# Two transformer blocks on one core: a feed-forward in three parts, with nine of 22 tile pairs as seven half-size products

## The chip, the cores and the metric

The kernel runs on one core of a Trainium2 chip. The metric is the device time in microseconds (us) of one execution. TensorE (PE) multiplies, VectorE (DVE) and ScalarE (ACT) work element by element, GpSimd (POOL) does a few copies, and SyncE (SP) issues most transfers; ScalarE and GpSimd can issue transfers too, each from a queue of its own.

## The reference

A sequence of 512 tokens with 1024 features goes through two blocks, in float32. The first block has three branches (a recurrent one, a latent attention, a differential attention with a position bias), a gated merge, an output product and a convolutional feed-forward. The second block has two layers; each is feed-forward, mixer, feed-forward:

```python
n = _modulate(_rmsnorm_2(h, norm_g[l, 0]), mod[:, 0, 0], mod[:, 0, 1])   # x * (1 + scale) + shift
h = h + 0.5 * mod[:, 0, 2] * _swiglu(n, ffn_w_in[l, 0], ffn_w_out[l, 0])

def _swiglu(x, w_in, w_out):                 # w_in 1024 x 5632, w_out 2816 x 1024
    a, b = jnp.split(x @ w_in, 2, axis=-1)
    return (jax.nn.silu(a) * b) @ w_out
```

`mod` comes from a vector c times `ada_w` (1024 x 9216 for each layer).

## The kernel before

Activations lie transposed: features on the 128 partitions in KD = 8 chunks, S = 512 tokens along a row. Each float32 operand is held as a pair `hi` + `lo` of float32r tiles; `mm3` multiplies three of the four combinations, so a 128 x 128 block of weights costs three matmuls of 512 columns. `weight` loads 128 x 1024 weights into `raw` (three buffers), makes `hi` on ScalarE and `lo = raw - hi` on VectorE (four buffers each). While the flag `spare` is set, every other `lo` is made on GpSimd.

`dense` makes one output tile of 128 features. `dense_halves` makes the first four of a stage in two halves of 256 tokens, so that they can start when the norm of the first half is there. `outputs` makes the last product of a stage and gathers the statistics of the next norm; its last tile (two tiles where the inner size is 8 chunks) is made in halves, and `part` computes the first half's norm factors during the second. `scaled` applies a norm.

`swiglu` has NF = 22 pairs of a gate tile and a value tile; `hh`, `hl` hold all 22 results, then 8 down tiles of 22 chunks each follow. There are four such feed-forwards, at about 1089, 1850, 2230 and 2970 us of the span. In each pair the gate goes through silu (L740), is multiplied with the value (L741) and split (L344, L346). `modulation` puts 72 products of `ada_w` (one 128 x 1024 transfer into `raw` and one VectorE operation, L1436) for each layer into a list from which `filler` takes them.

Order: a list scheduler places instructions on each engine's queue ahead of time by the order of the program, among those that it takes to be ready; a filler's instructions get a much lower priority. Each engine then works strictly through its own queue.

In the first block `filler` also interleaves the products that don't depend on a branch: `spilled` and `gates` write them to memory (`gates` after a tanh on ScalarE), and `gated` reads them back through SP's queue. `merge` sums the three gated branches; five of its eight tiles have two branches summed ahead (MERGED).

## Time and profile before

| | |
|---|---|
| median of 3 runs | 3353.23 us (3349.75 to 3354.49) |
| profiled execution | 3352.4 us, its span 3350.6 us |
| mean granted TensorE clock | 0.992 |
| TensorE busy | 98% of the span |
| VectorE, ScalarE, GpSimd busy | 57%, 40%, 2% |

The span runs from the first to the last instruction. Busy time of TensorE counts overlapping matmuls once, so a busy TensorE can still run below its rate: there the spacing of matmul starts is read from the timeline, and the granted clock from the windows.

### The profile page before, as it was taken

Reading aid. Unit: us, or ns where it says so; the run is one execution under the profiler, and the core shown is the slowest. Engines: PE = TensorE matmul, PEld = TensorE weight load, DVE = VectorE, ACT = ScalarE, POOL = GpSimd, SP = SyncE. Lnnn points to the kernel's source line nnn. Section 1 sums busy time; section 2 is a strip of 40 time slices with the busy share of each in tenths; the row PEclk is TensorE's granted clock in tenths of the full one; section 3 lists DMA queues with packets and bytes.
Section 4 is the critical chain, followed back from the end, with each engine's and each line's share of the span. In section 5 each row is a group of like instructions: output and inputs, shape, how many; then the busy total and the mean of one; then the engine's idle time right before and its main releaser. Section 6 shows DMA issues by size and latency. Waiting matters only on the chain.

```text
span 3350.6 us, 43133 instructions
## 1 busy us (share of the span) xinstructions
PE 3278.2 (98%) x16534; PEld 2724.2 (81%) x16534; DVE 1921.9 (57%) x3628; ACT 1346.7 (40%) x2365; POOL 79.7 (2%) x124
## 2 busy tenths in 40 slices
PE   8999998999999999999999999999999999999998
PEld 6779777788888888887787888898888878788887
DVE  6757685777664644368656644454444875653333
ACT  4646664444432322248632322232222774332321
POOL 0000121000000000000000000000000000000000
PEclk9999999999999999999999999999999999999999
DMA  5351225454453444441235444444443322423332
GB/s 180 94 148 36 81 90 177 154 153 156 139 170 122 138 149 136 146 127 61 88 108 186 137 139 148 143 125 140 149 150 125 94 76 89 153 89 100 95 93 71
DMA packets 144922, 415.00 MB, mean 124 GB/s; under 512 B 28005, under 2 KB 32933, under 8 KB 144202
## 3 DMA queue, kind: packets, MB, share of 16 engines
q1 hardware_dynamic: 142248, 408.02, 38.4%
q0 software_dynamic: 2176, 3.97, 0.5%
q8 instruction: 130, 2.13, 0.3%
q14 instruction: 78, 0.64, 0.1%
q10 hardware_dynamic: 290, 0.24, 0.0%
HBM read 383.06 MB, written 27.01 MB: 122 GB/s over the span
## 4 chain that ended last, share of the span: by engine, by line
PE 88%; DVE 5%; ACT 4%; DMA 2%; issue 1%; SPq 0%; DVEq 0%; ACTq 0%; POOL 0%; POOLq 0%
PE acc L277 25%; PE acc L279 25%; PE acc L278 25%; PE o L822 2%; PE s L783 2%; PE t L810 1%; PE s L278 1%; PE s L277 1%; PE s L279 1%; ACT hi L268 1%; DVE lo L272 1%; PE t L425 1%; DMA raw<-in_ada_dram 1%; PE s L1562 0%; ACT sq L1505 0%
## 5 line engine op out<-in xcount | busy, mean ns | idle before, releaser
L277 PE MATMUL acc<-xh,hi 128*128 128x512 f32 (+1 forms) x2872 | 1084.3, 381 | 17.1 <-ACT gst L627 3.6
L278 PE MATMUL acc<-xl,hi 128*128 128x512 f32 (+1 forms) x2872 | 1088.2, 381 | 2.5 <-DVE xl L348 1.2
L268 ACT ACTIVATE hi<-raw 128x1024 fp32r<-128x1024 f32 (+2 forms) x529 | 541.4, 1024 | 1361.4 <-PE acc L278 1247.0
L279 PE MATMUL acc<-xh,lo 128*128 128x512 f32 (+1 forms) x2872 | 1086.4, 381 | 1.1 <-DVE lo L272 1.1
L272 DVE TENSOR_TENSOR lo<-raw,hi 128x1024 fp32r<-128x1024 f32 (+1 forms) x513 | 613.0, 1196 | 462.3 <-ACT hi L268 440.0
L277 PEld LDWEIGHTS acc<-xh,hi 128*128 128x128 f32 x2872 | 541.1, 189 | 121.9 <-ACT gst L627 5.5
L278 PEld LDWEIGHTS acc<-xl,hi 128*128 128x128 f32 x2872 | 542.5, 189 | 101.1 <-issue 3.9
L279 PEld LDWEIGHTS acc<-xh,lo 128*128 128x128 f32 x2872 | 542.6, 189 | 98.6 <-issue 3.7
L1436 DVE CUSTOM_DVE_ANT_0 raw<-raw,sc,vp 128x1024 f32<-128x1024 f32 x144 | 184.9, 1284 | 269.4 <-DMA raw<-in_ada_dram 268.8
L279 PE MATMUL acc<-hh,lo 128*128 128x512 f32 (+1 forms) x880 | 338.0, 384 | 0.0
L278 PE MATMUL acc<-hl,hi 128*128 128x512 f32 (+1 forms) x880 | 334.5, 380 | 0.0
L277 PE MATMUL acc<-hh,hi 128*128 128x512 f32 (+1 forms) x880 | 333.0, 378 | 0.0
L278 PEld LDWEIGHTS acc<-hl,hi 128*128 128x128 f32 x880 | 165.2, 188 | 37.9
L277 PEld LDWEIGHTS acc<-hh,hi 128*128 128x128 f32 x880 | 165.1, 188 | 34.7
L279 PEld LDWEIGHTS acc<-hh,lo 128*128 128x128 f32 x880 | 165.4, 188 | 33.2
L741 DVE TENSOR_TENSOR g<-g,acc 128x512 f32<-128x512 f32 x84 | 57.8, 688 | 218.7 <-PE acc L279 217.8
L726 DVE SCALAR_TENSOR_TENSOR res<-acc,mod,res 128x512 f32<-128x512 f32 (+1 forms) x48 | 33.9, 707 | 120.0 <-PE acc L279 120.0
L346 DVE TENSOR_TENSOR ptl<-t,pth 128x512 fp32r<-128x512 f32 (+3 forms) x148 | 80.7, 566 | 29.8 <-ACT pth L344 28.8
L787 ACT ACTIVATE pr<-pr,mx 128x128 f32<-128x128 f32 (+3 forms) x160 | 88.7, 556 | 18.3 <-DVE mx L786 16.3
L786 DVE CUSTOM_DVE_ANT_0 pr<-s,cm 128x128 f32<-128x128 f32 (+3 forms) x160 | 75.0, 486 | 23.9 <-PE s L783 16.0
L344 ACT ACTIVATE pth<-t 128x512 fp32r<-128x512 f32 (+3 forms) x148 | 69.6, 496 | 40.4 <-PE t L810 37.3
L810 PE MATMUL t<-cm,pr 128*128 128x128 f32 x400 | 72.8, 276 | 2.5 <-DVE pr L796 2.5
(522 smaller groups left out, 4091.8 us busy)
## 6 DMA issues: line engine op xcount, KB each, us to landing
raw<-in_w_in_dram SPq DMA_DIRECT2D x176, 512.0 KB, 3.6
raw<-in_ada_dram SPq DMA_DIRECT2D x144, 512.0 KB, 3.5
raw<-in_w_out_dram SPq DMA_DIRECT2D x64, 512.0 KB, 3.5
raw<-in_w_mix_dram SPq DMA_DIRECT2D x56, 512.0 KB, 3.5
raw<-in_w_up_dram SPq DMA_DIRECT2D x44, 512.0 KB, 3.9
gd<-gst SPq DMA_DIRECT2D x56, 256.0 KB, 2.3
gt<-gd SPq DMA_DIRECT2D x56, 256.0 KB, 3.2
raw<-in_w_gate_dram SPq DMA_DIRECT2D x24, 512.0 KB, 4.1
```

The source lines that it names most:

```text
L268: self.last_act = nc.scalar.activation(hi[:, :n], raw[:, :n], AF.Copy)
L272: nc.vector.tensor_sub(lo[:, :n], raw[:, :n], hi[:, :n].bitcast(F32))
L277: return [mm(acc, ahi, bhi, start=start, stop=False, **kw), mm(acc, ahi, blo, start=False, stop=False, **kw), mm(acc, alo, bhi, start=Fals ...
L278: mm(acc, ahi, blo, start=False, stop=False, **kw),
L279: mm(acc, alo, bhi, start=False, stop=stop, **kw)]
L344: nc.scalar.activation(hi, src, AF.Copy, scale=scale)
L346: nc.vector.tensor_sub(lo, src, hi.bitcast(F32))
L783: nc.tensor.matmul(ps[:, :n], q[:, i * P:(i + 1) * P], kk[:, :n], start=k == 0, stop=k == len(passes) - 1)
L786: nc.vector.tensor_tensor_reduce(p, ps[:, :w], mask(i), -scale, 3.0e38, op0=OP.add, op1=OP.min, accum_out=mx[:, i:i + 1])
L787: nc.scalar.activation(p, p, AF.Exp, bias=mx[:, i:i + 1], scale=-1.0, accum_out=sm[:, i:i + 1])
L810: nc.tensor.transpose(ps[:, (i - j) * P:(i - j + 1) * P], probs[i][:, j * P:(j + 1) * P], self.c("ident"))
L1436: nc.vector.tensor_tensor_reduce(w, w, self.sc, 1.0, self.v("ada_b_2", l * 72 + n), op0=OP.mult, op1=OP.add, accum_out=self.mod[:, l, n:n ...
```

## The change

In the four feed-forwards of the second block:

- Nine of the 22 pairs (SEVEN) are made by `seven`. The value and gate tiles times the two halves of the features and the two halves of the tokens form a product of 2 x 2 blocks. It is made by seven products of half-size blocks (4 chunks, 256 columns) and additions, in place of eight. The additions on the weights are made for every pair on VectorE, those on the activations once for each feed-forward in `sums`, before pair 2. `scaled` keeps its rows in the buffers `sh`, `sl` for it (`keep`).
- The pairs go in three parts of 6, 8 and 8. After each part the 8 down tiles of that part's chunks are added to the residual. The first two down tiles of a part run all chunks but the last before either runs its last (`held`). The modulation products are taken two for each down tile instead of one for each pair.

In `outputs` with 8 chunks or fewer the last three tiles are made in halves, and the first two use `held`. In the first block and the mixer: the gates are written without tanh, and `gated` applies it after the load; several loads and stores move from SP's queue to GpSimd's or ScalarE's; `lo` is always made on VectorE; the merge order is 0 to 7 with 1, 2, 4, 5 and 7 summed ahead; in the third branch queries and keys are loaded one head ahead, and a head's normalisation (`normed`) follows later work; the bias rows come after the first unit's preparation; the key copies of the second branch are made once.

```diff
-    def swiglu(self, src_in, src_out, norm, gate):
+
+    PARTS = ((0, 6), (6, 14), (14, 22))
+    SEVEN = (3, 6, 8, 10, 12, 14, 16, 18, 20)
+    H = S // 2
+
+    def swiglu(self, src_in, src_out, norm, gate, shift4):
         nc, tc, t = self.nc, self.tc, self.t
+        H = self.H
         with tc.tile_pool(name="ffn", bufs=1) as pool:
+
+            th = t(pool, [P, 4, 4, H], F32R, "th")
+            tl = t(pool, [P, 4, 4, H], F32R, "tl")
+            xb = [t(pool, [P, 4, H], F32, n, 3) for n in ("sh", "sh", "sl", "sl")]
+            self.keep = lambda k, a: xb[k // 4 * 2 + (a > 0)][:, k % 4]
             norm()
-            hh = t(pool, [P, NF, S], F32R, "hh")
-            hl = t(pool, [P, NF, S], F32R, "hl")
-            for f in range(NF):
-                if f == 0:
-                    accs = self.dense_halves([src_in[0], src_in[NF], src_in[1], src_in[NF + 1]])
-                ga, va = (accs.pop(0) if accs else self.dense(src_in[n], KD, self.xh, self.xl) for n in (f, NF + f))
-                g = t(pool, [P, S], F32, "g", 2)
-                nc.scalar.activation(g, ga, AF.Silu)
-                nc.vector.tensor_mul(g, g, va)
-                self.split(hh[:, f], hl[:, f], g)
-                self.filler(1, self.mods)
-            self.outputs(src_out, NF, hh, hl, self.residual(gate), None, 2)
+            self.keep = None
+            hh = t(pool, [P, 8, S], F32R, "hh")
+            hl = t(pool, [P, 8, S], F32R, "hl")
+            accs = self.dense_halves([src_in[0], src_in[NF], src_in[1], src_in[NF + 1]])
+            for p, (f0, f1) in enumerate(self.PARTS):
+                for f in range(f0, f1):
+                    i = f - f0
+                    if f == 2:
+                        self.sums(xb, th, tl, shift4)
+                    if f not in self.SEVEN:
+                        ga, va = (accs.pop(0) if accs else self.dense(src_in[n], KD, self.xh, self.xl) for n in (f, NF + f))
+                        g = t(pool, [P, S], F32, "g", 2)
+                        nc.scalar.activation(g, ga, AF.Silu)
+                        nc.vector.tensor_mul(g, g, va)
+                        self.split(hh[:, i], hl[:, i], g)
+                    else:
+                        self.seven(pool, src_in[f], src_in[NF + f], th, tl, hh[:, i], hl[:, i])
+                kc = f1 - f0
+                cols = slice(f0 * P, f1 * P)
+                down = [src_out[n][:, cols] for n in range(KD)]
+                if p < len(self.PARTS) - 1:
+                    put = self.residual(gate)
+                    two = self.held(down[:2], kc, hh, hl)
+                    for n in range(KD):
+                        acc = two[n] if n < 2 else self.dense(down[n], kc, hh, hl)
+                        put(n, slice(0, S), acc)
+                        self.filler(2, self.mods)
+                else:
+                    self.outputs(down, kc, hh, hl, self.residual(gate), None, 2)
...
+    def sums(self, b, th, tl, shift4):
+
+
+        nc, H = self.nc, self.H
+        s1, s2 = shift4(0), shift4(4)
+        ds = self.t(self.np_, [P, 4], F32, "ds", 1)
+        nc.vector.tensor_sub(ds, s2, s1)
+        nc.vector.tensor_sub(b[0], b[0], b[1])
+        nc.vector.tensor_sub(b[2], b[3], b[2])
+        nc.vector.tensor_add(b[2], b[2], b[0])
+        stt = nc.vector.scalar_tensor_tensor
+        for k in range(4):
+            stt(b[1][:, k], b[3][:, k], ds[:, k:k + 1], b[1][:, k], op0=OP.add, op1=OP.subtract)
+            stt(b[3][:, k], b[3][:, k], s2[:, k:k + 1], b[0][:, k], op0=OP.add, op1=OP.add)
+        self.split(th[:, 0], tl[:, 0], b[0])
+        self.split(th[:, 3], tl[:, 3], b[3], -1.0)
+        self.split(th[:, 1], tl[:, 1], b[1])
+        self.split(th[:, 2], tl[:, 2], b[2])
+
+    def raw(self, src):
+        raw = self.t(self.wp, [P, self.WN], F32, "raw", 3)
+        self.nc.sync.dma_start(raw, src)
+        return raw
+
+    def seven(self, pool, src_g, src_v, th, tl, hi, lo):
+
+
+        nc, t, H = self.nc, self.t, self.H
+        ra, rb = self.raw(src_g), self.raw(src_v)
+        W = self.WN
+        g1, g2, v1, v2 = ra[:, :W // 2], ra[:, W // 2:], rb[:, :W // 2], rb[:, W // 2:]
+        def parts(pool, tags, src, bufs):
+            x = [t(pool, [P, W], F32R, n, bufs) for n in tags]
+            n = src.shape[-1]
+            self.split(x[0][:, :n], x[1][:, :n], src)
+            return x
+
+        ah, al = parts(self.wp, ("hi", "lo"), ra, 4)
+        bh, bl = parts(self.wp, ("hi", "lo"), v2, 4)
+
+        nc.vector.tensor_add(v2, v1, v2)
+        nc.vector.tensor_add(v1, g1, v1)
+        nc.vector.tensor_add(g1, v2, g1)
+        nc.vector.tensor_add(g2, g1, g2)
+        ch, cl = parts(pool, ("sh", "sl"), ra, 3)
+        dh, dl = parts(pool, ("sh", "sl"), rb, 3)
+
+        def product(acc, wh, wl, half, xs):
+            for k in range(4):
+                s = slice(half * (W // 2) + k * P, half * (W // 2) + (k + 1) * P)
+                self.mm3(acc, wh[:, s], wl[:, s], xs[0][:, k], xs[1][:, k], k == 0, k == 3)
+
+        X = lambda k, h: [x[:, 4 * k:4 * k + 4, h * H:(h + 1) * H] for x in (self.xh, self.xl)]
+        T = lambda i: (th[:, i], tl[:, i])
+        two = lambda x: x.rearrange("p (a b) -> p a b", b=H)
+        twice = lambda x: x[:, None, :].to_broadcast([P, 2, H])
+        add = nc.vector.tensor_add
+        p17, p26 = self.bank("s"), self.bank("s")
+        p45, p3 = self.bank("t"), self.bank("t")[:, :H]
+        v = t(self.np_, [P, S], F32, "nm", 2)
+        q = t(pool, [P, H], F32, "q", 2)
+        g = t(pool, [P, S], F32, "g", 2)
+        product(p17[:, :H], ah, al, 0, X(0, 0))
+        product(p17[:, H:], dh, dl, 0, T(1))
+        product(p26[:, :H], ah, al, 1, X(1, 0))
+        product(p26[:, H:], ch, cl, 0, T(3))
+        y = t(self.np_, [P, S], F32, "sqa")
+        nc.scalar.activation(y, p17, AF.Copy)
+        add(two(g), twice(y[:, :H]), two(p26))
+        add(q, g[:, H:], y[:, H:])
+        product(p45[:, :H], bh, bl, 0, T(2))
+        product(p45[:, H:], dh, dl, 1, T(0))
+        add(two(v), twice(q), two(p45))
+        product(p3, ch, cl, 1, X(1, 1))
+        add(g[:, H:], g[:, H:], p45[:, H:])
+        add(g[:, H:], g[:, H:], p3)
+        nc.scalar.activation(g, g, AF.Silu)
+        nc.vector.scalar_tensor_tensor(g, v, -1.0, g, op0=OP.mult, op1=OP.mult)
+        self.split(hi, lo, g)
...
+    def held(self, srcs, kc, xh, xl):
+
+        ws = [self.weight(src, kc * P) for src in srcs]
+        accs = [self.bank("acc") for _ in ws]
+        for k0, k1 in ((0, kc - 1), (kc - 1, kc)):
+            for (hi, lo), acc in zip(ws, accs):
+                for k in range(k0, k1):
+                    s = slice(k * P, (k + 1) * P)
+                    self.mm3(acc, hi[:, s], lo[:, s], xh[:, k], xl[:, k], k == 0, k == kc - 1)
+        return accs
...
-        last = range(KD - (2 if kc <= 8 else 1), KD)
+        last = range(KD - (3 if kc <= 8 else 1), KD)
+        n0 = 0
+        if kc <= 8:
+
+            accs = self.held(src[:2], kc, xh, xl)
+            n0 = 2
         for n in range(last[0]):
-            acc = self.dense(src[n], kc, xh, xl)
+            acc = accs[n] if n < n0 else self.dense(src[n], kc, xh, xl)
...
-        if self.spare and self.n % 2:
-            nc.gpsimd.tensor_sub(lo[:, :n], raw[:, :n], hi[:, :n].bitcast(F32))
-        else:
-            nc.vector.tensor_sub(lo[:, :n], raw[:, :n], hi[:, :n].bitcast(F32))
+        nc.vector.tensor_sub(lo[:, :n], raw[:, :n], hi[:, :n].bitcast(F32))
...
+                if self.keep is not None:
+                    m = self.keep(k, a)
+                else:
+                    if b - a == S or k % 2 == 0:
+                        m2 = self.place() if self.place else self.t(self.np_, [P, S], F32, "nm", 2)
...
-            nc.sync.dma_start(g, gd[(b0 + i) * KD + n])
+            nc.gpsimd.dma_start(g, gd[(b0 + i) * KD + n])
+            kw = {} if self.gbias is None else {"bias": self.gbias[:, (b0 + i) * KD + n:(b0 + i) * KD + n + 1]}
+            nc.scalar.activation(g, g, AF.Tanh, scale=0.5, **kw)
...
-        for n in [*range(done, KD), *range(done)]:
-            if n < done:
+        for n in range(KD):
+            if n in done:
                 p = self.t(pool, [P, S], F32, "gb", 3)
-                nc.sync.dma_start(p, before[n])
+                nc.gpsimd.dma_start(p, before[n])
...
-            r = self.factors(acc, 0, S, P, 1e-5, "s")
+            self.filler((2, 1, 1, 1)[h])
+            return h, o, acc
+
+        def normed(h, o, acc):
+
+            with tc.issue_after(self.last_mm.ins):
+                r = self.factors(acc, 0, S, P, 1e-5, "s")
             nc.vector.scalar_tensor_tensor(o, o, sub, r, op0=OP.mult, op1=OP.mult)
             self.split(out[0][:, h], out[1][:, h], o)
-            self.filler((2, 2, 1, 0)[h])
-
+
+        def loads(h):
+
+            q = t(pool, [P, S], F32, "qz", 2)
+            nc.gpsimd.dma_start(q, self.zd[2 * h])
+            k = t(pool, [P, 2, S], F32, "kz", 2)
+            for i in range(2):
+                nc.gpsimd.dma_start(k[64 * i:64 * i + 64], self.zd[2 * h + 1].rearrange("(m r) c -> r m c", m=2))
+            return q, [k[:, m] for m in range(2)]
...
+        ahead = loads(0)
         rooms = [t(self.xp, [P, KD * S], F32, n) for n in ("xh", "xl")]
         for h in range(4):
 
             room = rooms[h % 2]
             bias = room[:, :1280]
             nc.sync.dma_start(bias, self.bias_d[bass.ds(self.odd, 1), h])
-            qacc = t(pool, [P, S], F32, "qz", 2)
-            nc.sync.dma_start(qacc, self.zd[2 * h])
+            qacc, kaccs = ahead
+            if h < 3:
+                ahead = loads(h + 1)
...
+                with tc.issue_after(self.turn.ins) if h == m == 0 else nullcontext():
+                    prs.append(self.scores(pool, room[:, (1 + m) * 1280:(2 + m) * 1280], [(qs, kh), (qs, kl)],
+                                           lambda i: bias[:, off[i]:off[i + 1]], 1.0))
+                if m == 0 and h > 1:
+                    normed(*done)
             if h:
-                finish(h - 1, before)
+                done = finish(h - 1, before)
             before = prs
-        finish(3, before)
+        normed(*done)
...
-                    self.bias_regular(bp)
+                    rows = self.bias_regular(bp, pp)
                 for u in range(2):
                     self.rwkv_prep(pp, u, st[u], Ls, ab, pwpa, tw, w2a2, w2w0, a0h, r0 if u == 0 else None)
-                    self.filler(2)
+                    if u == 0:
+                        self.bias_rows(*rows)
+                    self.filler(3 - u)
             self.rwkv_solve(sp, Ls, st)
-            self.filler(7)
+            self.filler(6)
```

## Rows read from the trace of the kernel before

**Rows 1.** The page: busy time of each engine, and the chain that ended last.

```profile
PE 3278.2 (98%) x16534; PEld 2724.2 (81%) x16534; DVE 1921.9 (57%) x3628; ACT 1346.7 (40%) x2365; POOL 79.7 (2%) x124
...
PE 88%; DVE 5%; ACT 4%; DMA 2%; issue 1%; SPq 0%; DVEq 0%; ACTq 0%; POOL 0%; POOLq 0%
```

**Rows 2.** Windows: first feed-forward of the second block, rising and down part.

```profile
core 0: us, PE busy (x) PEld busy (x) DVE busy (x) ACT busy (x) POOL busy (x), PEclk, DMA share, GB/s
1114.00:1331.00 217.00, 217.00 (x960) 179.67 (x959) 101.21 (x124) 64.94 (x81) 0.00 (x0) 1.00 0.48 153
1331.00:1449.00 118.00, 118.00 (x547) 96.79 (x545) 45.57 (x55) 26.98 (x31) 0.00 (x0) 1.00 0.40 129
```

**Rows 3.** Timeline, TensorE: 256-column matmuls; start, length, engine, line, operands.

```profile
1439.95 0.29 PE L278 MATMUL acc<-hl,hi 128*128 128x256 f32 x1
...
1441.99 0.28 PE L277 MATMUL acc<-hh,hi 128*128 128x256 f32 x1
```

**Rows 4.** Timeline, TensorE: 512-column matmuls of a down tile.

```profile
1400.04 0.40 PE L279 MATMUL acc<-hh,lo 128*128 128x512 f32 x1
...
1411.94 0.40 PE L279 MATMUL acc<-hh,lo 128*128 128x512 f32 x1
```

**Rows 5.** Groups by form, 1114 to 1331 us: busy, mean ns, idle before.

```profile
L272 DVE TENSOR_TENSOR lo<-raw,hi 128x1024 fp32r<-128x1024 f32 x40 | 48.9, 1223 | 14.4 <-ACT hi L268 12.7
...
L1436 DVE CUSTOM_DVE_ANT_0 raw<-raw,sc,vp 128x1024 f32<-128x1024 f32 x21 | 27.0, 1284 | 52.5 <-DMA raw<-in_ada_dram 52.5
...
L346 DVE TENSOR_TENSOR hl<-g,hh 128x512 fp32r<-128x512 f32 x20 | 13.7, 686 | 0.0
```

**Rows 6.** Groups by form, VectorE, whole span.

```profile
L504 DVE SCALAR_TENSOR_TENSOR xl<-nm,mod,xh 128x256 fp32r<-128x256 f32 x96 | 43.1, 480 | 0.0
...
L726 DVE SCALAR_TENSOR_TENSOR res<-acc,mod,res 128x512 f32<-128x512 f32 x40 | 30.0, 751 | 97.0 <-PE acc L279 97.0
```

**Rows 7.** Timeline, VectorE: last operations of the norm, four feed-forwards.

```profile
1106.23 1.26 DVE L766 SCALAR_TENSOR_TENSOR res<-res,vp,t 128x256 f32<-128x256 f32 x3
...
1863.69 0.48 DVE L504 SCALAR_TENSOR_TENSOR xl<-nm,mod,xh 128x256 fp32r<-128x256 f32 x1
...
2234.59 0.88 DVE L504 SCALAR_TENSOR_TENSOR xl<-nm,mod,xh 128x256 fp32r<-128x256 f32 x2
...
2984.44 1.22 DVE L272 TENSOR_TENSOR lo<-raw,hi 128x1024 fp32r<-128x1024 f32 x1
```

**Rows 8.** Timeline, TensorE: first matmul of pair 2, four feed-forwards.

```profile
1114.03 0.40 PE L277 MATMUL acc<-xh,hi 128*128 128x512 f32 x1
...
1876.40 0.40 PE L277 MATMUL acc<-xh,hi 128*128 128x512 f32 x1
...
2243.38 0.40 PE L277 MATMUL acc<-xh,hi 128*128 128x512 f32 x1
...
2995.62 0.40 PE L277 MATMUL acc<-xh,hi 128*128 128x512 f32 x1
```

**Rows 9.** Windows: start of the second feed-forward; columns as in rows 2.

```profile
1850.00:1855.00 5.00, 4.39 (x21) 4.28 (x21) 5.00 (x22) 2.44 (x5) 0.00 (x0) 0.50 0.22 84
```

**Rows 10.** Windows: second and third branch, merge, and a mixing output.

```profile
365.00:500.00 135.00, 126.23 (x610) 97.70 (x609) 104.91 (x217) 89.83 (x195) 30.90 (x29) 0.99 0.26 85
500.00:570.00 70.00, 62.73 (x365) 53.92 (x363) 35.52 (x81) 35.57 (x76) 11.84 (x5) 0.98 0.57 180
570.00:630.00 60.00, 54.26 (x276) 42.80 (x276) 46.35 (x144) 31.80 (x77) 0.05 (x1) 0.92 0.30 95
630.00:665.00 35.00, 33.38 (x132) 26.58 (x132) 20.47 (x32) 9.36 (x14) 0.56 (x1) 0.89 0.71 239
1805.00:1850.00 45.00, 42.60 (x234) 37.14 (x234) 26.96 (x51) 14.85 (x21) 0.00 (x0) 0.96 0.43 131
```

**Rows 11.** Chain of waits: two transfers; start, length, what.

```profile
69.27 6.21 DMA nm<-gvd
...
509.15 5.65 DMA kz<-sp
```

More of the change, by code (lines that the diff above doesn't have):

```diff
@@ L207, in __init__ @@
         self.fill, self.mods, self.made = [], [], set()
[L208 to L209 removed]
+        self.last_act = self.last_mm = self.turn = self.place = None
+        self.keep = None
         nc = tc.nc
@@ L537, in block1 @@
             nc.scalar.dma_start(self.vp[:, n:], A["vp"][:, n:])
-            self.first = [self.bank("acc" if i < 3 else "s") for i in range(len(self.FIRST))]
+            self.first = [self.bank(n) for n in ("acc", "acc", "s", "s", "t")]
             def product(i, k):
@@ L594, in two @@
                 nc.sync.dma_start(m01[n], self.gated(n, pool, gd, [o_rwkv, o_mla], A["w_br"], 0))
-            self.fill += [lambda n=n: two(n) for n in range(self.MERGED)]
+            self.fill += [lambda n=n: two(n) for n in self.MERGED]
             self.diff(pool, o_diff)
```

113 lines of the change are left out of this document (54 added, 59 removed).

## The prediction

> **What bounds the kernel now.** I read the page first: TensorE (PE) is busy for 98% of the span and the chain of waits runs 88% over it, nearly all in the three matmuls of `mm3` [rows 1]. VectorE (DVE) is busy 57%. Time can therefore come from two places only: fewer TensorE columns, or the few per cent in which TensorE waits or runs at the lower clock. The windows by stage come next. In the feed-forward's rising part (20 plain pairs) and its down part TensorE has no idle time and the granted clock is 1.00, while DVE works for 101 of 217 us and 46 of 118 us [rows 2]. So in that stretch the price of a TensorE instruction is paid in full, and DVE has 116 us free in which new additions can hide, as long as they come in time. Last the timeline, for the spacing of matmuls, which is their cost (durations of neighbours overlap).
>
> **The seven products.** The window of 217 us holds 960 matmuls of 512 columns, 0.226 us each [rows 2]. A plain pair has 2 tiles x 8 chunks x 3 = 48: 10.85 us. At 256 columns 17 spacings take 1441.99 - 1439.95 = 2.04 us, 0.120 each [rows 3], and this with a weight load before every one, as the seven products will have. Seven products x 4 chunks x 3 = 84 matmuls: 10.08 us. A replaced pair saves 0.77 us; 9 pairs in 4 feed-forwards are 36: **-27.7 us**. Seven eighths of 10.85 would be 9.49: half-size matmuls give back 0.59 of the 1.36 us. The Trainium skill ("TensorE: Matmul & The Clock Gate", section Back-to-back issue gap) gives 262 cycles for 256 columns and 518 for 512; by that estimate at 2.4 GHz the pair would go from 10.36 to 9.17 us and the 36 would save 43 us. The trace does not agree for these float32r matmuls (0.120 us is 288 cycles), and the row decides.
>
> **What the products cost VectorE.** Per replaced pair: three splits of 1024 columns at 1.22, one of 512 at 0.69, four additions of 512 at 0.69; after the products five full-width and two or three half-width operations, about 3.8 us in all (lengths as in [rows 5], half width 0.48 in [rows 6]). Sum 10.9 us, against 3.8 for a plain pair (2 x 1.22, 2 x 0.69). A replaced and a plain pair together have 14.7 us of DVE work in 20.9 us of TensorE time. DVE follows, with 6 us to spare. The operands of the next replaced pair need its second raw buffer: a transfer (I allow 6 us, as the two of [rows 11]), then splitting and adding of some 8 us, in the 20.9 us between two replaced pairs: I cost it at nothing. Its cover is the plain pair in between; without it, the wait is rival three.
>
> **The sums at f == 2.** `sums` stands before the weights of pair 2. It has three additions of 1024 (1.2 each), eight operations of 256 at 0.39 (three of them take 1.26 in [rows 7]) and four splits of 1024 (1.2): 11.6 us of DVE. Before it in program order stand the norm and the four operations that end pairs 0 and 1 (2.7); behind it stand the weight remainders `lo` of pair 2 (first one 1.2), on which TensorE's next product waits. DVE comes out of the norm at 1107.5, 1864.2, 2235.5 and 2985.7 us [rows 7]; adding 15.5 gives 1123.0, 1879.7, 2251.0 and 3001.2. TensorE wants pair 2 at 1114.0, 1876.4, 2243.4 and 2995.6 [rows 8]. The waits would be 9.0, 3.3, 7.6 and 5.6: 25.5 us. The other end is nothing: DVE's order isn't the program's order (ready operations go ahead of ones that wait for ScalarE), so `lo` may slip in front. The sums' own operations are mostly independent of each other and fill such gaps themselves, so I take rather more than half: **+14**. After a gap TensorE runs at the lower of its two levels, 1.2 GHz: from 1850 to 1855 us, behind such a gap, the granted clock is 0.50 [rows 9]. Five us at half speed cost 2.5, at most 10 for the four waits; I take **+4**.
>
> **The three parts.** The down part's matmul count stays (528 full-width ones per feed-forward, counting two halves as one). Its last pair is covered: two tiles' first chunks, 30 or 42 matmuls, 7 to 10 us, run before the held chunk is read, and a pair's tail is 0.6 + 0.7 + 0.6 + 0.7 us. Sixteen more residual additions (0.75, [rows 6]) and the modulation products (1.28, [rows 5]), which move from the rising part to the down tiles, two per tile, bring a first-part tile to 0.9 + 0.75 + 2.6 = 4.2 us of DVE beside 18 x 0.233 = 4.2 of TensorE; as the modulation has the lowest priority it can run over into the rising part, where 6 us are free in every 21. Each of parts two and three begins with a replaced pair whose value weights get their buffer when only two down tiles are left (8.4 or 11 us), against some 8 us of preparing: between 0 and 2 us per start, eight starts, taken as **+4** (0 to 16). Down matmuls now stand (1411.94 - 1400.04) / 51 = 0.233 apart [rows 4], those of the rising part 0.226. Both read the same weight buffers; only the moving tile differs. If the smaller `hh` tile took the faster spacing, 4 x 456 x 0.007 = 13 us would come back; nothing says that it does, so I take 0.
>
> **The ends of the short products** (`outputs` with 8 chunks: the block's output and both mixing outputs) now hold three tiles instead of two, 72 half matmuls or 8.6 us of second half over the first half's statistics in place of 48 or 5.8. At one of these ends TensorE is idle 2.4 of 45 us at clock 0.96, another 1.8 us [rows 10]. **-3** for the three, from -8 to +2 (one more weight buffer is held).
>
> **The first block.** Its waits are visible: from 365 to 665 us TensorE idles 8.8, 7.3, 5.7 and 1.6 us, and the clock of 0.98, 0.92 and 0.89 costs another 1.4, 4.8 and 3.9 [rows 10]; two more lie on the chain of waits as transfers, 6.2 us before the bias rows and 5.6 before the first scores of the third branch [rows 11]. The change touches most of these places: the bias rows go behind other work and to GpSimd's queue, the third branch's queries and keys are fetched one head ahead, the normalisation of a head waits behind later matmuls, key copies are made once, GpSimd's weight remainders go to DVE (1.2 each, DVE is 78% busy there), the merge interleaves short and long columns. Of about 40 us I take a third, **-13**, between -28 (most of it) and +4 (DVE now late in the second branch). The Trainium skill ("DMA: Bandwidth & Descriptors", Issuing engines are not separate DMA queues) says that another issuing engine saves only the issuing; by that alone this term would lie near 0, inside these bounds. The gates' tanh moves to the merge, 56 operations of about 0.6 us on ScalarE, which idles most of it: 0, at worst +3.
>
> **Sum.** -27.7 + 14 + 4 + 4 - 3 - 13 = -21.7. The profiled execution took 3352.4, within 1 us of the median 3353.23: 3352.4 - 21.7 = **3331 us**.
>
> **Rivals.**
> 1. *The sums hide.* The remainders of pair 2 go ahead of the additions, the parts start in time, and the first block gives most of its waits back: -27.7 + 2 - 6 - 25 = -57, **3296 us**. For it: DVE has 116 free us per rising part [rows 2]. Against it: program order puts the additions first.
> 2. *All is given back.* The waits at pair 2 come in full with the slow clock (25.5 + 10), the part starts cost 12, the first block gives 13 and the ends 3: -27.7 + 35.5 + 12 - 16 = +3.8, **about 3356 us**. For it: the free DVE time is not where the sums stand [rows 7, 8].
> 3. *Operands late, slower than before.* In every replaced pair the second product waits for the last split of the summed weights, the end of a chain of transfer, split, four additions, split. It decides against the change from 0.6 us of lateness per pair (21.7 / 36); with 2 us it is 36 x 2 = 72 on top: **3403 us**. For it: three raw buffers only, two of them held through the chain. Against it: 20.9 us of room for a chain of about 14.
>
> **How the numbers follow.** Forecast (3312 to 3346) 0.55; rival one 0.22; rival two 0.13; rival three 0.10. The range leaves out rival three and the far halves of one and two: 3294 to 3349. A change of 0.2% (6.7 us) is about what measurement can tell. Rival two lies on both sides: 0.05 faster, 0.06 the same, 0.02 slower. Faster 0.55 + 0.22 + 0.05 = 0.82, same 0.06, slower 0.12.
>
> **What will show it.** Replaced pairs 10.1 us apart from plain ones at 10.9: right products. TensorE's idle time just before pair 2, released by `lo`: the sums; none there: rival one. Idle time inside each replaced pair, released by the split of summed weights: rival three. Down matmuls 0.226 apart would add 13 us of gain. Windows from 365 to 665 us with clock near 1 and less idle time: the first block. I am wrong if the half-size products stand more than 0.129 us apart (10.85 / 84), or if DVE runs without a gap through the rising part.

## The result and the profile after

The changed kernel takes 3374.48 us (median, 3373.67 to 3378.14) against 3351.49 (3348.56 to 3354.49) for the kernel before: ratio 1.0069, 95% interval 1.0057 to 1.0081. It is slower by 0.7%, 23 us; the prediction was 3331 us. The profiled execution has a span of 3372.0 us and a mean granted clock of 0.984 (3350.6 and 0.992 before).

In its numbering `mm3` is L274 to L276, the remainder of `weight` L269, the two steps of `split` L359 (ScalarE) and L361 (VectorE), the loads of `seven` L797, its additions L816 to L819, the residual L728, the modulation L1577 (load) and L1578 (VectorE), and at the end of a stage the statistics product L440 (TensorE), the last step of the norm's factor `rsy` L410 (VectorE) and the product that spreads it L448 (TensorE).

The first rows are the page's busy times, to be held against [rows 1]. TensorE is busy for 10 us less, VectorE for 329 us more. The span still grew by 21 us, so TensorE waits more or runs slower.

```profile
PE 3268.0 (97%) x17926; PEld 2786.6 (83%) x17926; DVE 2251.0 (67%) x4191; ACT 1479.2 (44%) x2555; POOL 95.3 (3%) x196
```

The start of each stage's last residual row (L728; in the conv feed-forward L724) divides the span:

| us | before | after | difference |
|---|---|---|---|
| to the end of the conv feed-forward | 1084.5 | 1077.6 | -6.8 |
| four feed-forwards | 372.4, 371.8, 367.0, 367.8 | 381.1, 375.0, 378.0, 369.1 | +24.3 |
| two mixers | 390.6, 384.5 | 389.6, 388.3 | +2.9 |
| tail | 12.2 | 13.3 | +1.1 |

The first row is one execution of each kernel and no price: in the experiments that keep the first block's edits and leave the conv feed-forward as it is, its end lies between 1070.7 and 1084.0 us. Experiment 8 prices it.

**The products are as cheap as computed.** Timeline of TensorE within a replaced pair: 25 spacings in 2.98 us, 0.119 each, no wait between (first fence); and a window of one replaced and one plain pair (second fence, columns as in [rows 2]): 21 us without idle time, clock 1.00, 14.0 us of VectorE (14.7 were computed). Down matmuls (third fence) keep 0.233: 51 spacings in 11.90 us, as in [rows 4].

```profile
1225.49 0.28 PE L274 MATMUL s<-th,sh 128*128 128x256 f32 x1
...
1228.47 0.28 PE L275 MATMUL t<-tl,sh 128*128 128x256 f32 x1
```

```profile
1246.00:1267.00 21.00, 21.00 (x135) 19.11 (x135) 14.04 (x19) 8.65 (x11) 0.00 (x0) 1.00 0.32 100
```

```profile
1300.06 0.39 PE L274 MATMUL acc<-hh,hi 128*128 128x512 f32 x1
...
1311.96 0.40 PE L274 MATMUL acc<-hh,hi 128*128 128x512 f32 x1
```

**What TensorE waits for**, summed over the span (us in total, times, longest). The first two rows have no counterpart of this size before; the third and fourth belong to the norm's first use after a short product.

```profile
PE acc L276 <- DVE lo L269: 14.9, 4, 7.8
PE s L274 <- ACT sh L359: 13.5, 3, 4.9
...
PE acc L274 <- ACT xh L521: 6.6, 5, 1.5
PE o L448 <- DVE rsy L410: 4.6, 5, 0.9
```

*Before pair 2.* VectorE in the first feed-forward: four splits of the sums end, and only then come the two `lo` of pair 2. TensorE (second fence) had the `hi` products of pair 2 behind it and stood for 7.76 us. In the windows (third fence; columns as in [rows 2]) the clock is 1.00 before, 0.72 over the gap and 0.59 in the seven us after it, between the two levels (1.00 and 0.50), as in [rows 9]. The other three feed-forwards wait 2.4 us each; after these equal waits the clock is 1.00 in the second and 0.58 and 0.76 in the third and fourth (last fence).

```profile
1112.45 1.22 DVE L361 TENSOR_TENSOR tl<-sh,th 128x1024 fp32r<-128x1024 f32 x1
1113.59 1.22 DVE L361 TENSOR_TENSOR tl<-sl,th 128x1024 fp32r<-128x1024 f32 x1
1114.72 1.22 DVE L363 SCALAR_TENSOR_TENSOR tl<-sl,th 128x1024 fp32r<-128x1024 f32 x1
1115.86 2.35 DVE L269 TENSOR_TENSOR lo<-raw,hi 128x1024 fp32r<-128x1024 f32 x2
```

```profile
1117.13 0.80 PE L276 MATMUL acc<-xh,lo 128*128 128x512 f32 x1 [7.76 <-DVE lo L269]
```

```profile
1100.00:1109.00 9.00, 8.23 (x63) 7.51 (x62) 8.66 (x14) 4.45 (x6) 0.00 (x0) 1.00 0.27 60
1109.00:1117.00 8.00, 0.38 (x2) 0.17 (x2) 8.00 (x12) 2.60 (x3) 0.00 (x0) 0.72 0.00 0
1117.00:1124.00 7.00, 6.87 (x19) 5.44 (x20) 4.82 (x7) 0.63 (x1) 0.00 (x0) 0.59 0.49 150
```

```profile
1882.00:1889.00 7.00, 7.00 (x31) 5.80 (x32) 4.79 (x7) 2.18 (x3) 0.00 (x0) 1.00 0.42 150
2256.60:2264.00 7.40, 7.37 (x20) 5.80 (x21) 4.32 (x5) 0.63 (x1) 0.00 (x0) 0.58 0.44 142
3022.80:3030.00 7.20, 7.20 (x25) 5.75 (x26) 4.28 (x5) 1.07 (x2) 0.00 (x0) 0.76 0.44 146
```

*Before pair 6*, the replaced pair that opens part two. SP (DMA issues; where two are joined, the second starts at the end of the length less 0.33) issues its two weight loads (L797) only after the last modulation loads of part one, the second at 1188.2, when VectorE has reduced the row that held the buffer (second fence; the third is SP's own wait for that reduction). The weights are there at 1192.6, 4.4 us later; the split of summed weights runs from 1198.5 (fourth) and TensorE waits 3.73 us (fifth). After it the clock is 0.66 (sixth). In the fourth feed-forward, where the modulation list is used up, this wait is absent.

```profile
1182.52 1.53 SPq L1577 DMA_DIRECT2D raw<-in_ada_dram  x2
1185.81 2.74 SPq L797 DMA_DIRECT2D raw<-in_w_in_dram  x2
```

```profile
1186.90 1.28 DVE L1578 CUSTOM_DVE_ANT_0 raw<-raw,sc,vp 128x1024 f32<-128x1024 f32 x1 [0.46 <-DMA raw<-in_ada_dram]
```

```profile
SPq L797 <- DVE mod L1578: 2.0, 1, 2.0
```

```profile
1192.67 0.63 ACT L359 ACTIVATE hi<-raw 128x512 fp32r<-128x512 f32 x1 [1.40 <-DMA raw<-in_w_in_dram]
...
1198.51 1.06 ACT L359 ACTIVATE sh<-raw 128x1024 fp32r<-128x1024 f32 x1 [3.40 <-DVE raw L819]
```

```profile
1200.57 0.39 PE L274 MATMUL s<-th,sh 128*128 128x256 f32 x1 [3.73 <-ACT sh L359]
```

```profile
1196.00:1201.00 5.00, 1.27 (x11) 1.06 (x10) 4.50 (x7) 2.28 (x3) 0.00 (x0) 1.00 0.30 105
1201.00:1206.00 5.00, 5.00 (x31) 5.00 (x30) 2.10 (x2) 1.78 (x3) 0.00 (x0) 0.66 0.77 233
```

*The first block*, the four windows of [rows 10] that lie in it: less idle time in the first and the last, the same in the other two, and a lower clock there (0.95 and 0.83 against 0.98 and 0.92). The windows are fixed in time, so the work in them is shifted by a few us.

```profile
365.00:500.00 135.00, 130.90 (x640) 102.03 (x640) 111.80 (x252) 92.36 (x200) 6.54 (x12) 1.00 0.30 94
500.00:570.00 70.00, 62.71 (x376) 54.83 (x375) 40.98 (x95) 42.31 (x94) 8.63 (x15) 0.95 0.59 174
570.00:630.00 60.00, 54.24 (x254) 43.12 (x255) 43.71 (x132) 31.12 (x70) 6.93 (x13) 0.83 0.35 115
630.00:665.00 35.00, 34.66 (x149) 27.49 (x148) 25.71 (x36) 18.16 (x26) 6.43 (x12) 1.00 0.65 200
```

### The profile page after: what moved, and what is told of

Its sections match the earlier page's. It is cut to its first block, busy times and chain, and to the rows that moved or that the text cites. A ratio compares the mean times of both kernels' runs of the same rounds, so it can differ in the third digit from the quotient of the medians.

```text
span 3372.0 us, 46619 instructions
## 1 busy us (share of the span) xinstructions
PE 3268.0 (97%) x17926; PEld 2786.6 (83%) x17926; DVE 2251.0 (67%) x4191; ACT 1479.2 (44%) x2555; POOL 95.3 (3%) x196
## 5 line engine op out<-in xcount | busy, mean ns | idle before, releaser
L274 PE MATMUL acc<-xh,hi 128*128 128x512 f32 (+1 forms) x2296 | 862.9, 381 | 20.1 <-ACT gst L644 6.9
L276 PE MATMUL acc<-xh,lo 128*128 128x512 f32 (+1 forms) x2296 | 862.7, 379 | 15.4 <-DVE lo L269 14.9
L275 PE MATMUL acc<-xl,hi 128*128 128x512 f32 (+1 forms) x2296 | 862.3, 379 | 1.4 <-DVE xl L522 0.7
L268 ACT ACTIVATE hi<-raw 128x1024 fp32r<-128x1024 f32 (+4 forms) x456 | 462.6, 1017 | 843.6 <-PE acc L275 575.5
L269 DVE TENSOR_TENSOR lo<-raw,hi 128x1024 fp32r<-128x1024 f32 (+4 forms) x456 | 533.1, 1172 | 310.8 <-ACT hi L268 296.6
L274 PEld LDWEIGHTS acc<-xh,hi 128*128 128x128 f32 x2296 | 436.9, 192 | 101.3 <-ACT gst L644 8.8
L276 PEld LDWEIGHTS acc<-xh,lo 128*128 128x128 f32 x2296 | 438.5, 191 | 90.4 <-DVE lo L269 15.7
L275 PEld LDWEIGHTS acc<-xl,hi 128*128 128x128 f32 x2296 | 437.7, 191 | 74.0 <-issue 2.5
L276 PE MATMUL acc<-hh,lo 128*128 128x512 f32 (+1 forms) x880 | 334.2, 380 | 0.0
L274 PE MATMUL acc<-hh,hi 128*128 128x512 f32 (+1 forms) x880 | 334.1, 380 | 0.0
L1578 DVE CUSTOM_DVE_ANT_0 raw<-raw,sc,vp 128x1024 f32<-128x1024 f32 x144 | 184.1, 1283 | 83.6 <-DMA raw<-in_ada_dram 82.8
L274 PEld LDWEIGHTS acc<-hh,hi 128*128 128x128 f32 x880 | 165.2, 188 | 34.9
L276 PEld LDWEIGHTS acc<-hh,lo 128*128 128x128 f32 x880 | 165.3, 188 | 34.7
L728 DVE SCALAR_TENSOR_TENSOR res<-acc,mod,res 128x512 f32<-128x512 f32 (+1 forms) x112 | 78.0, 706 | 136.6 <-PE acc L276 136.6
L359 ACT ACTIVATE hi<-raw 128x512 fp32r<-128x512 f32 x73 | 61.4, 842 | 137.5 <-DMA raw<-in_w_in_dram 53.4
L361 DVE TENSOR_TENSOR lo<-raw,hi 128x512 fp32r<-128x512 f32 x73 | 69.5, 954 | 75.0 <-ACT hi L359 72.8
L274 PE MATMUL s<-xh,hi 128*128 128x256 f32 x416 | 118.1, 284 | 0.9 <-DVE g L759 0.5
L276 PE MATMUL s<-xh,lo 128*128 128x256 f32 x416 | 118.2, 284 | 0.7 <-DVE lo L361 0.7
L275 PE MATMUL s<-xl,hi 128*128 128x256 f32 x416 | 118.1, 284 | 0.0
```

What stands on the lines that cost most here:

```text
L268: self.last_act = nc.scalar.activation(hi[:, :n], raw[:, :n], AF.Copy)
L269: nc.vector.tensor_sub(lo[:, :n], raw[:, :n], hi[:, :n].bitcast(F32))
L274: r = [mm(acc, ahi, bhi, start=start, stop=False, **kw), mm(acc, ahi, blo, start=False, stop=False, **kw), mm(acc, alo, bhi, start=False, ...
L275: mm(acc, ahi, blo, start=False, stop=False, **kw),
L276: mm(acc, alo, bhi, start=False, stop=stop, **kw)]
L359: nc.scalar.activation(hi, src, AF.Copy, scale=scale)
```

## The experiments

Each kernel was timed in turn with the kernel before on the same chip. The last column is (ratio - 1) x 3351.5 us, so that runs of different hours can be compared; intervals are 0.0009 to 0.0017 to either side, so a difference of two rows is known to some 4 to 7 us. The changed kernel stands at 1.0069, +23.

| experiment | median us | ratio (95%) | us against before |
|---|---|---|---|
| 1 sums one pair later | 3351.47 | 0.9996 (0.9987 to 1.0005) | -1 |
| 2 modulation beside plain pairs | 3391.73 | 1.0116 (1.0101 to 1.0130) | +39 |
| 3 two tiles in halves | 3355.69 | 1.0013 (1.0004 to 1.0023) | +4 |
| 4 feed-forward of before | 3348.25 | 0.9990 (0.9982 to 0.9999) | -3 |
| 5 no replaced pairs | 3359.80 | 1.0019 (1.0010 to 1.0028) | +6 |
| 6 = 1 + 3 | 3330.18 | 0.9928 (0.9915 to 0.9942) | -24 |
| 7 = 6, modulation in the conv | 3321.49 | 0.9905 (0.9890 to 0.9920) | -32 |
| 8 = 4 + 3 | 3340.49 | 0.9965 (0.9954 to 0.9975) | -12 |
| 9 = 6, modulation spread | 3311.34 | 0.9882 (0.9866 to 0.9899) | -40 |
| 10 modulation loads on GpSimd | 3386.80 | 1.0107 (1.0090 to 1.0124) | +36 |
| 11 = 9, no replaced pairs | 3341.17 | 0.9961 (0.9947 to 0.9975) | -13 |
| 12 = 9, three tiles | 3333.31 | 0.9932 (0.9919 to 0.9946) | -23 |

**1. Sums one pair later.**

```diff
-    SEVEN = (3, 6, 8, 10, 12, 14, 16, 18, 20)
+    SEVEN = (4, 6, 8, 10, 12, 14, 16, 18, 20)
...
-                    if f == 2:
+                    if f == 3:
                         self.sums(xb, th, tl, shift4)
```

> The sums over halves are issued one pair later (at f == 3), and the first replaced pair becomes pair 4 instead of pair 3; nothing else changes. Theory 1 (the weight splits of pair 2 stand behind the sums on VectorE, and the waits before pair 2 with the half clock after them cost 11.4 + 3.0 + 5.9 + 4.7 = 25 us in the four feed-forwards of the changed kernel): about 3374 - 25 = 3350 us, no wait of over 1 us of TensorE's 512-column products for the second weight's low half before pair 2, and at most 1 us before pair 3, since pair 2's 21.7 us of products now cover the sums. Rival A (the sums take VectorE whatever pair they stand before, so the wait only moves to pair 3): 3374 us, the same waits 21.7 us later. Rival B (half of it moves): 3362 us.

24 us less than the changed kernel, as theory 1 said (25). The row of `lo` L269 is gone from the largest waits; that of pair 6 stays, and now leads them (TensorE's waits):

```profile
PE s L274 <- ACT sh L359: 13.0, 3, 5.9
PE acc L274 <- ACT gst L644: 10.3, 5, 3.3
```

**2. Modulation beside the plain pairs.**

```diff
                         self.split(hh[:, i], hl[:, i], g)
+                        if f > 6:
+                            self.filler(2, self.mods)
...
-                        self.filler(2, self.mods)
+                        self.filler(2 if p else 0, self.mods)
```

> The 16 modulation rows that each feed-forward issues beside the down tiles of its first part are issued beside the plain pairs from pair 7 on, two at each; their number and all else stay. Theory 1 (part two's first replaced pair, pair 6, is late because its two weight loads and its splits and adds stand behind modulation loads on SP and modulation reductions on VectorE): the waits before pair 6 in the first three second-block feed-forwards (5.5 + 6.6 + 8.2 = 21 us with the half clock after them) go, from pair 3's silu to pair 6's 65.4 us as in the fourth, and the time is about 3374 - 20 = 3354 us. Rival A (a replaced pair at the start of a part is late by itself, its operands being long to prepare): waits stay at 4 to 5 us, 3374 us. Rival B (the modulation makes the same wait wherever it stands, now before pairs 8 to 20): 3374 us, with new waits there.

Theory 1 is right about the place and wrong about the sum: in the first feed-forward the wait before pair 6 is gone (silu of pair 3 to that of pair 6 in 66.2 us), but the kernel is 16 us slower. Rival B: the waits come back elsewhere and grow. Two new groups stand among TensorE's waits, one inside replaced pairs and one in down tiles:

```profile
PE s L276 <- DVE sl L361: 7.7, 9, 1.3
...
PE acc L274 <- DVE res L728: 7.4, 4, 2.3
```

SP shows why (the load in `seven` is L799 here, the modulation's L1579): after a modulation load it issues nothing for 5.7 us until a buffer is free, and the next pair's weights come after that.

```profile
1333.37 0.33 SPq L1579 DMA_DIRECT2D raw<-in_ada_dram  x1
1339.11 1.47 SPq L799 DMA_DIRECT2D raw<-in_w_in_dram  x2
```

**3. Two tiles in halves** at the ends of the short products, with the turns of before.

```diff
-        last = range(KD - (3 if kc <= 8 else 1), KD)
+        last = range(KD - (2 if kc <= 8 else 1), KD)
...
-                self.part(0, behind[n + (14 if kc <= 8 else 9)], behind[n + (40 if kc <= 8 else 30)])
+                self.part(0, behind[n + 9], behind[n + 30])
```

The edit reaches seven ends: the block's output, both mixing outputs and, since their third part has 8 chunks, all four feed-forwards.

> The ends of the short products (the feed-forward's last part and the mix's product) split two tiles into halves instead of three, with the norm's two turns at products 9 and 30 of the second half as in the kernel before. Theory 1 (with three tiles the first half's norm factor comes later than the weight splits leave VectorE free, and TensorE idles 1.1 + 1.7 us with a half clock after, at each of the four starts behind a short product): 1.5 to 3 us each, 3374 - 9 = about 3365 us. Rival A (the three-tile end gains what was predicted, 3 us in all, and the late start is from VectorE alone): 3377 us or more. Rival B: no difference within 3 us.

19 us less, twice the expectation: theory 1 had the right sign, and its 1.5 to 3 us at each of four starts were too little. The stages say where: mixers 385.2 and 383.5 (389.6 and 388.3), the second to fourth feed-forwards 2 to 3 us less each. A stage begins with the wait that the end before it leaves, so the mixers' share belongs to ends of feed-forwards.

**4. The feed-forward of before** in the changed kernel (`swiglu` replaced by the old one, all else kept).

> The changed kernel with the second block's feed-forward of the kernel before (22 plain pairs, one part, 22 chunks to a down tile, the modulation beside the pairs); the edits in the first block, the ends of the mix's products and the held chunk there stay. Theory 1 (stage by stage: the first block and the conv feed-forward gained 6.8 us, and all of the loss is in the four feed-forwards, +24.3 us, with +4 in the mixes and the tail): 3374 - 24 - 3 = about 3346 us, faster than the kernel before by 4 to 7 us. Rival A (the first block's gain is an accident of one execution): 3351 us. Rival B (the prediction's first-block term of 13 us is right and something else hides it): 3339 us.

Theory 1 within 2 us: the loss sits in the feed-forward.

**5. No replaced pairs**: SEVEN is empty and `sums` isn't called; three parts, three-tile ends and modulation stay.

> No pair is replaced and the sums over halves are left out; the three parts, the held chunks, the three-tile ends, the modulation beside the down tiles and the first block's edits stay. Theory 1 (the 36 replaced pairs do save 36 x 0.77 = 27.7 us, the sums cost the 23 us that their move gave back, and pair 6's wait of 4 to 5 us shrinks to about 2 because a plain pair needs fewer splits before it): 3374 + 28 - 23 - 8 = about 3371 us. Rival A (the products save little in the time, their gain lost in waits inside the replaced pairs): 3374 - 23 - 8 = 3343 us. Rival B (the parts are the whole loss): 3400 us.

Between theory 1 and rival A, 11 us under the first. The reason is in the stages: part two takes 132.1 and 131.9 us in the first two feed-forwards and 131.9 in the fourth, where no modulation is left, so there a plain pair 6 is not late; theory 1 had left 2 us. (In the third feed-forward pair 6 waits 1.3 us.) Three parts of plain pairs with these ends cost 6 us over the kernel before although the first block gives 12 (experiment 8).

**6. Sums later and two tiles** (edits 1 and 3 together).

> The changed kernel with the sums one pair later (first replaced pair 4) and with two tiles in halves at the ends of the short products. Theory 1 (two separate costs): 3374 - 23 - 19 = 3332 us, 0.6 % under the kernel before. Rival A (both relieve the same busy VectorE at the feed-forward's start, so half of the second gain is lost): 3341 us. Rival B (only the larger counts): 3351 us.

Theory 1: 47 us less than the changed kernel, 24 and 19 being the parts. The two costs are separate.

**7. The same, and the modulation moved**: none beside part one's down tiles, one beside each plain pair from 7 on, two in place of one beside each pair of the conv feed-forward.

> As the kernel with the sums one pair later and two tiles in halves, and the modulation taken off the first part's down tiles: 22 more of its rows beside the conv feed-forward's pairs (two at each) and one beside each plain pair from pair 7 on. Theory 1 (pair 6 waits for loads behind modulation; one row per plain pair leaves the three load buffers free in time, where two made waits of 1 to 4 us): 3332 - 18 = about 3314 us. Rival A (two rows beside a conv pair make the same waits as two beside a plain pair, 1 us and more at each of 22): 3335 us. Rival B (one row per pair already costs, 1 us at each of 24): 3335 us as well, with the waits in the second block.

8 of the 18 us arrived. The four feed-forwards fell from 1471.8 to 1449.2 us, but the profiled first block ended at 1093.1 in place of 1080.2, with ten waits of 0.4 to 1.0 us, 6.6 in all, of the conv's tiles for their own VectorE work. The one lies outside the 1070.7 to 1084.0 us of the other runs.

**8. The feed-forward of before and two tiles** (edits 3 and 4): what the edits outside the second block's feed-forward are worth.

> The changed kernel with the feed-forward of the kernel before and two tiles in halves at the ends of the mix's products: what the first block's edits are worth alone. Theory 1 (the three-tile end costs some 4 us where a norm follows the mix): 3348 - 5 = 3343 us, 8 us under the kernel before. Rival (the three-tile end costs only where the feed-forward itself ends on it): 3348 us.

-12 us, 8 less than with three tiles: theory 1.

**9. Sums later, two tiles, modulation spread.**

```diff
                         self.split(hh[:, i], hl[:, i], g)
+                        if f > 6:
+                            self.filler(1, self.mods)
...
-                        self.filler(2, self.mods)
+                        self.filler(2 if p else int(n < 5), self.mods)
```

> As the kernel with the sums one pair later and two tiles in halves, with one modulation row at each of the first five down tiles of part one (instead of two at all eight), and one beside each plain pair from pair 7 on; the conv feed-forward has one per pair again. Theory 1 (the kernel with the modulation in the conv feed-forward gained 22.6 us in the four feed-forwards and lost about 10 of it in that stage): the feed-forwards stay at about 1450 us, the first block returns to about 1079: 3321 - 10 = about 3311 us. Rival A (five rows ahead of pair 6's loads still make it wait, 2 us with the half clock in each of three feed-forwards): 3318 us. Rival B (the later first block was one execution's accident): 3321 us.

3311.34 us, as theory 1 said, and **faster than both kernels: 1.2% under the one before**. TensorE at pair 2 and at the start of part two, the windows that answer to those of the changed kernel: almost no idle time, clock 1.00.

```profile
1109.40:1119.40 10.00, 9.41 (x44) 7.68 (x43) 10.00 (x12) 4.07 (x5) 0.00 (x0) 1.00 0.17 48
1182.00:1192.00 10.00, 10.00 (x84) 9.91 (x83) 6.88 (x10) 3.35 (x4) 0.00 (x0) 1.00 0.68 224
```

**10. The modulation's loads issued by GpSimd** in the changed kernel (`nc.sync` becomes `nc.gpsimd` in `modulation`).

> The changed kernel with one edit: the modulation rows' loads are issued by GpSimd instead of SP; their number, place, buffers and reductions stay. Theory 1 (pair 6's weights wait for one of the three load buffers that they share with the modulation, each held until VectorE has reduced its row): the waits before pair 6 stay at 4 to 5 us in the first three feed-forwards, within 5 us of 3374. Rival A (the loads of pair 6 stand behind the modulation's in SP's own order): the waits go, 3354 us. Rival B (the issue on GpSimd is dearer and later): over 3380 us.

The wait before pair 6 did not go, so SP's order isn't what makes it (rival A falls). The time is the one of rival B (over 3380 us). With no modulation load before them on SP, the two loads of pair 6 still start late, the second again 2.4 us behind the first:

```profile
1183.66 0.33 SPq L265 DMA_DIRECT2D raw<-in_w_out_dram  x1
1189.05 2.74 SPq L797 DMA_DIRECT2D raw<-in_w_in_dram  x2
```

What holds the second is the buffer: SP waits for the modulation's reduction there, as in the changed kernel. The 12 us more over the changed kernel go beyond theory 1; the same waits became longer (15.4 us in four), and by the stages the first two feed-forwards took 4.5 and 6.7 us more. An issue lasts 0.53 us on GpSimd against 0.33 on SP, but what makes the 12 us was not tested further.

**11. Experiment 9 without its products**: all pairs plain, no sums, the modulation at the same places.

> The kernel at 3311 us (sums one pair later, two tiles in halves, modulation spread) without its products: all 22 pairs plain, no sums over halves, the modulation at the same 8 pairs and tiles. What the replaced pairs are worth with no wait around them. Theory 1 (0.77 us for each of 36 pairs): 3311 + 28 = 3339 us. Rival A (about 1.0 us a pair, as the fourth feed-forward's 364.1 against 373.1 us reads): 3347 us. Rival B (the products gain nothing and all of the difference to the changed kernel is in the three waits): 3311 us.

The products are worth 26 us (0.0079 of 3351.5), known to some 7, 0.74 a pair: theory 1, and rival A's 36 us lie outside. The fourth feed-forward, which has no wait in either kernel, took 367.8 against 360.0 us, 0.87 a pair; the runs don't tell 0.77 from 0.87. And three parts of plain pairs (-13) are no dearer than one part (-12, experiment 8).

**12. Experiment 9 with three tiles in halves.**

> The kernel at 3311 us with three tiles in halves at the ends of the short products, as in the change, instead of two. Theory 1 (the three-tile end has a cost of its own, 5 us in the feed-forwards, 9 in the mixes, 1 at the tail): 3311 + 15 to 19 = about 3328 us. Rival A (it mattered only beside the crowded VectorE of the changed kernel): 3311 to 3316 us.

17 us more: the three-tile end costs by itself, whatever VectorE has to do beside it. At the end of the first mixer, VectorE (first fence experiment 12, second 9): with three tiles the first half's norm factor `rsy` is ready at 1842.98, 1 us *after* the start of the last residual row, its steps mixed with remainders `lo` of the next weights; with two it is ready at 1824.2, 3.5 us *before* that row.

```profile
1839.67 1.22 DVE L269 TENSOR_TENSOR lo<-raw,hi 128x1024 fp32r<-128x1024 f32 x1
...
1842.05 0.48 DVE L728 SCALAR_TENSOR_TENSOR res<-t,mod,res 128x256 f32<-128x256 f32 x1 [0.29 <-PE t L276]
...
1842.82 0.16 DVE L410 SCALAR_TENSOR_TENSOR rsy<-rsw,rsy 128x2 f32<-128x2 f32 x1
```

```profile
1824.07 0.16 DVE L410 SCALAR_TENSOR_TENSOR rsy<-rsw,rsy 128x2 f32<-128x2 f32 x1
...
1827.71 0.48 DVE L728 SCALAR_TENSOR_TENSOR res<-s,mod,res 128x256 f32<-128x256 f32 x1
```

Most of the delay arises before VectorE, in TensorE's queue. The statistics product L440, from which the factor is computed, has its last input (`sq` of the first half) at 1833.5 us and starts at 1838.2, behind 49 of the second half's 72 products (third fence); with two tiles it starts when its input is there, behind 10 of 48 (fourth). VectorE's steps then last 3.8 us against 1.9. By these numbers an L440 right behind the 15th product, where the code lets it go, would have given the factor at about 1839 (an estimate: 1834.1 + 1.0 + 3.8).

```profile
1833.10 0.42 ACT L476 ACTIVATE sq<-res 128x256 f32<-128x256 f32 x1 [2.46 <-DVE res L728]
...
1838.08 0.28 PE L274 MATMUL t<-xh,hi 128*128 128x256 f32 x1
1838.20 0.28 PE L440 MATMUL t<-ones,sqa 128*128 128x1 f32 x2
```

```profile
1820.90 0.42 ACT L476 ACTIVATE sq<-res 128x256 f32<-128x256 f32 x1 [2.46 <-DVE res L728]
...
1821.32 0.28 PE L440 MATMUL t<-ones,sqa 128*128 128x1 f32 x2
```

Why it stands so late was not tested. It follows the first product of the third tile, which takes its accumulator from the group `t`, the one that the statistics use too; and the experiment changed the tiles, that accumulator and the two turns (behind the 15th and 41st product against the 10th and 31st) together.

The windows from the last residual row on, six us each, experiment 12 and then 9: 2.5 us idle and a clock of 0.85 and 0.87 against 0.4 us and 1.00.

```profile
1842.00:1848.00 6.00, 3.53 (x22) 3.06 (x21) 5.57 (x22) 2.81 (x5) 0.00 (x0) 0.85 0.47 170
1848.00:1854.00 6.00, 6.00 (x47) 6.00 (x46) 6.00 (x17) 3.83 (x8) 0.00 (x0) 0.87 0.01 3
```

```profile
1827.70:1833.70 6.00, 5.58 (x44) 5.36 (x45) 5.29 (x24) 3.74 (x8) 0.00 (x0) 1.00 0.21 82
1833.70:1839.70 6.00, 6.00 (x53) 6.00 (x52) 6.00 (x16) 2.70 (x7) 0.00 (x0) 1.00 0.00 0
```

## Why the prediction was wrong

| term | predicted | measured | by |
|---|---|---|---|
| 36 replaced pairs | -27.7 | -26 | 9 against 11 |
| first block (and the other edits outside) | -13 | -12 | 8 |
| sums, waits and clock | +14 + 4 | +24 | 1 |
| three parts, starts | +4 | +15 | 9 against 6 |
| ends of the short products | -3, for three ends | +17 to +19, at seven | 12 against 9; 3 |
| of these, the three ends that were counted | -3 | +8 | 4 against 8 |
| sum | -21.7 | +18 to +20 | +23 in the whole kernel |

The line of the three counted ends is part of the one above it and not added again. The measured terms add up to the whole within their intervals.

**Right.** The price of the products, from the spacing of matmuls [rows 2, 3], held to about a us, in a difference known to some 7. The Trainium skill ("TensorE: Matmul & The Clock Gate", Back-to-back issue gap) gives its cycles for a matmul by itself; the estimate from them, 43 us, is refuted by the 26 measured. Rival three (operands late in every replaced pair) does not happen.

**Right in size, in part by luck: the first block.** It came out at a third of the visible waits. But of the sign that was to show it, only half came: in its four windows TensorE idles 5.9 us less in all, while the clock costs some 2 us more (two windows have a lower one). Where the rest of the 12 us comes from, and which of the edits gave how much, is open. The Trainium skill ("DMA: Bandwidth & Descriptors", Issuing engines are not separate DMA queues) says that issuing from several engines saves only the issuing. By that the term would lie near 0; the -12 does not fit, but the first block's edits are not only queues, so the rule isn't tested.

**Wrong in sign, and counted at three of seven places: the ends of the short products.** The step looked at the idle time that a longer second half could cover [rows 10] and treated the third tile as more cover. It took only "the block's output and both mixing outputs"; but the third part of a feed-forward has 8 chunks and ends in the same `outputs`, so four more ends are held in three halves. And it did not ask when the first half's factor would be made. With three tiles it is ready after the second half, and the next norm begins with an idle TensorE. The row of L448 among its waits has five such places, three behind a feed-forward (at 1459.8, 2224.3 and 2602.3 us) and two behind a mixer. Even the three counted ends cost 8 us where 3 were to be gained. "One more weight buffer is held" was not the reason: the statistics product stands late in TensorE's queue, and VectorE's mixed rows add 1.9 us (experiment 12). Why the scheduler puts it there was not shown.

**Mis-sized: the starts of the parts.** "Between 0 and 2 us per start, eight starts" was 4 to 5 us at three of them and nothing at the other five. The step set 8.4 us of cover (two down tiles) against "some 8 us of preparing". The changed kernel has just these: from the issue of the value weights to the moment when TensorE wants the split 8.6, 7.4 and 7.1 us before pair 6 of the first three feed-forwards. But the product on that split starts 12.4, 12.3 and 12.1 us after the issue, since the weights first take 4.3 to 4.5 us to land. This transfer, for which the prediction allowed 6 us inside a part, was left out at the starts. Part three begins with 13.1 and 12.6 us of cover where modulation stands before it, and just escapes. The cover is so short because modulation, down weights and pair 6's weights share the three `raw` buffers: where no modulation is left (pair 6 of the fourth feed-forward) the same load is issued 20.5 us ahead. Low priority doesn't help there: a row already loaded holds its buffer until it is reduced. Experiments 2, 9 and 10 bear this out: in experiment 6 the three waits are 14.2 us, and moving the modulation (9) gave back 15.

**Mis-sized: the clock behind the waits.** The waits of pair 2 were 14.9 us against the +14 taken. That is nearer than its terms (7.8 and three times 2.4, not the 9.0, 3.3, 7.6 and 5.6 worked out), and of its two reasons only one held: the sums did fill gaps (the first runs at 1102.5 us, among operations of pairs 0 and 1), while `lo` did not slip in front. Moving the sums gave back 24, so some 9 us, known to about 5, lie beside the visible waits; +4 was taken for the clock and 10 called the most. The windows behind the four waits show 2.9, 0, 3.1 and 1.7 us of it.

So of the three rivals the second, "all is given back" (3356), was nearest. The kernel was 18 us slower than that: the ends alone lie 20 us above its -3, its 35.5 for pair 2 was 11 too much.

## What to carry to other kernels

Where the bottleneck engine has no idle time, its saved instructions are worth what their spacing says; what decides is the side work, and it has to be asked for each new batch of it *which operation of the next tile is queued behind it and which buffer it holds*. Placing the same work otherwise (sums one pair later, modulation spread, two tiles in place of three) turned +0.7% into -1.2% without changing a product. Count a helper's callers before you price an edit in it. Price a wait of the matmul engine with the slow stretch after it: here 14.9 us of waits came to 24.

## What was not expected of the hardware

- Idle times of 0.4 to 0.6 us left the granted clock at 1.00 in the windows shown (experiment 9); where TensorE idled 2.5, 3.7 and 7.8 us, windows in and behind the gaps have 0.85 and 0.87, 0.66, and 0.72 and 0.59. But the length of the gap does not settle it: behind three waits of 2.4 us each, before pair 2, the clock was 1.00, 0.58 and 0.76. Why is open.
- The spacing of full-width matmuls differs with what moves: 0.233 us from `hh` tiles in both kernels [rows 4], 0.226 from `xh` [rows 2], though `hh` is now a third of its size. What makes the difference was not tested.
